# Gate and up of the 128-slot experts in blocks of 1024 columns over four PSUM banks

## The chip, the core and the metric

The kernel runs on one core of one Trainium2 chip, as one launch. The metric is the device time of that launch in microseconds (us), and each time named for a kernel is the median of several executions. The profiler took one more execution apart; its rows are used below. Engines are named as the profile names them: PE is TensorE, DVE is VectorE, ACT is ScalarE, POOL is GpSimd, and SP is SyncE, which here issues the weight transfers.

## What is computed

The reference is two stacks of transformer layers over 256 tokens of width 1024 in fp32. The change touches only the last feed-forward layer, a mixture of eight experts of which each token takes two:

```python
def swiglu_2(x, wg, wu, wd):
    return (jax.nn.silu(x @ wg) * (x @ wu)) @ wd

def moe_swiglu(x, router, wg, wu, wd):
    ...
    logits = (t @ router).astype(jnp.float32)
    top_v, top_i = lax.top_k(logits, TOP_K)
    ...
    for e in range(N_EXPERTS):
        y = y + gate[:, e:e + 1] * swiglu_2(t, wg[e], wu[e], wd[e]).astype(jnp.float32)
```

For each expert `wg` and `wu` are 1024 x 3584 and `wd` is 3584 x 1024, all fp32: 44.0 MB for an expert, 352 MB for the eight.

## The kernel before

**Jobs.** `moe` (line 2303) runs the eight experts one after the other in the order of `JOBS`: L, S, L, L, S, L, L, S. An L job has 128 slots for tokens (five experts), an S job 64 (three experts). The tokens of an expert are gathered by a selection matrix on PE, and its result is added back to the sum in the same way (`scatter`).

**An L job** (`job_l`, line 2371). Weights come in units of 128 x 1024 fp32, which is 512 KB. A unit lands in a raw buffer and is split by ACT (`hi`, rounded to fp32r) and DVE (`lo`, the rest). There are eight pairs of `hi` and `lo`. A product takes three fp32r matmuls of 512 columns: x hi by w hi, x hi by w lo, x lo by w hi. Gate and up are done by `stream_gu` (line 2257) in seven blocks j of 512 columns. A block takes two PSUM banks, one for gate and one for up, and 48 matmuls: eight k, three products, two weights. One unit holds 512 columns of two neighbouring k, so each of its rows of DRAM is 2 KB long. At a block's end ACT takes silu of the gate bank and DVE multiplies it by the up bank (`evac_gu`). A side task then transposes the result on PE in another bank and splits it. The down product is a `stream` of 28 units, 168 matmuls in two banks.

**An S job** uses the weights as they land, in fp32 matmuls on half of PE's columns (line 330). Its gate and up already come as units of 128 x 1024 of one k in three blocks, and as two-k units for the last 512 columns.

**Banks.** Of the eight PSUM banks four (`mq`) serve the main streams and four (`sm`) the side tasks: transposes, gathers, scatters. `lend(n)` (line 360) moves banks between the two.

**The order** of the instructions is fixed when the program is written out, by a planner in the kernel. It keeps a clock for PE, one for each other engine and one for the transfers, with a price for each operation; for the transfers it is 358e3 bytes a us (line 206). A matmul is written out when the planner thinks that its operands and its bank are ready (`pe` and `until`, line 263). Splits of units go into ACT's and DVE's queues up to 8 us (`AHEAD`) ahead of the planner's clock.

**Fillers.** Where the planner thinks that PE will stand idle for 1.2 us or more and a bank has been free for that long, `reach` (line 273) writes out matmuls of the identity, 128 x 128 in fp32, into a free bank: as many as cover the planned gap but for its last us. Nobody reads what they make. They are the matmuls of line 286:

```python
        while self.pe_end + 1.0 < self.clock:
            self.nc.tensor.matmul(ps[:, 0:128], self.c["ident"], self.c["ident"], start=True, stop=True)
            self.pe_end += 0.214
```

They are part of PE's queue, so PE runs them whether or not the gap is there on the chip.

Of the kernel before, what the change touches and what calls it, by code (L numbers as in the profile page):

```python
# [19 lines left out]
S, D, KD = 256, 1024, 8  # L20
# [95 lines left out]
class Net:  # L116
# [526 lines left out]
    def xf(self, t, k):  # L643
        self.wait(self.evs[t][k // 4])
        return self.xT[t][0][:, k], self.xT[t][1][:, k]
# [1367 lines left out]
    def plan_moe(self):  # L2013
        A = self.A

        g, u, d = (A[f"moe_w_{z}_2"][0].rearrange("e (c p) f -> p (e c) f", p=128) for z in ("gate", "up", "down"))
        self.m_val = {}

        def two(w, i, c, js):

            def get():
                b = self.expert(i)[0] if i is not None else None
                z = w[:, c:c + 2, js] if b is None else w[:, bass.ds(b + c, 2), js]
                return [z[:, 0, :], z[:, 1, :]], z
            return get

        def one(w, i, c, js, which):
            def get():
                b = self.expert(i)[which] if i is not None else None
                z = w[:, c:c + 1, js] if b is None else w[:, bass.ds(b + c, 1), js]  # L2030
                return [z[:, 0, :]], None
            return get

        for path, i in self.JOBS:
            plain = path == "S"
            for b in range(3 if plain else 0):
                for k in range(KD):
                    for w in (g, u):
                        self.unit(one(w, i, k, slice(b * 1024, b * 1024 + 1024), 0), plain=True)
            for j in range(6 if plain else 0, 7):  # L2040
                for k in range(0, KD, 2):
                    for w in (g, u):
                        self.unit(two(w, i, k, slice(j * 512, j * 512 + 512)), plain=plain)
            for k in range(28):
                self.unit(one(d, i, k, slice(0, 1024), 1), plain=plain)

# [199 lines left out]
    def stream(self, n, xf, evac):  # L2246
# [7 lines left out]
        evac(ps)  # L2254
        self.mq.put(2)

    def stream_gu(self, xf, evac):

        ps = self.new_mm()
        for k in range(KD):  # L2260
            if k % 2 == 0:
                ids = [self.take(), self.take()]
            xh, xl = xf(k)
            for a, (l, r) in enumerate(((xh, 0), (xh, 1), (xl, 0))):
                for z, i in enumerate(ids):
                    self.mm(ps[:, z * 512:z * 512 + 512], l, self.units[i][r][:, k % 2 * 512:k % 2 * 512 + 512],
                            k == 0 and a == 0, k == KD - 1 and a == 2)
            if k % 2:
                for i in ids:
                    self.done(i)  # L2270
            self.pump()
        evac(ps)
        self.mq.put(2)
# [29 lines left out]
    def moe(self, result, before):  # L2303
# [32 lines left out]
        def at_down(n, k):  # L2336

            if k == 12 and n < 7:
                path, i = self.JOBS[n + 1]
                self.spawn((self.gather if path == "L" else self.gather_s)(i, Gs[n + 1]))  # L2340
            if k == 10 and n == 7:
                wb.extend(before())
                self.wait(sev[6])
                self.grab(self.sm, 4)
                for t in range(2):
                    fin.append([self.new_sm() for _ in range(2)])
                    for h in range(2):
                        self.mm(fin[t][h], c["ident"], yacc[t][h], True, False)

        def scatter(n, lhs, yh, yl, back):  # L2350

            if n == 7:
                for t in range(2):
                    for h in range(2):
                        self.mm(fin[t][h], lhs(t, h), yh[h], False, False)
                        self.mm(fin[t][h], lhs(t, h), yl[h], False, True)
                self.fire(sev[n])
                return
            yield self.at(*yh, *yl)
            for t in range(2):  # L2360
                for h in range(2):
                    yield (self.sm, 1)
                    p2 = self.new_sm()
                    self.mm(p2, lhs(t, h), yh[h], True, False)
                    self.mm(p2, lhs(t, h), yl[h], False, True)
                    v.tensor_add(yacc[t][h], yacc[t][h], p2)
                    self.sm.put()
            self.blk.put(back)
            self.fire(sev[n])

        def job_l(n, G):
            hT, hev = [None] * 7, [Ev() for _ in range(7)]

            def xf(k):
                self.wait(G["ev"][k // 4])
                hi, lo = G["x"][k // 4]
                return hi[:, (k % 4) * 128:(k % 4) * 128 + 128], lo[:, (k % 4) * 128:(k % 4) * 128 + 128]

            def evac_gu(j):
                def go(ps):  # L2380
                    self.grab(self.blk, 2)
                    sg, h = self.new_blk(), self.new_blk()
                    nc.scalar.activation(sg, ps[:, 0:512], AF.Silu)
                    v.tensor_mul(h, ps[:, 512:1024], sg)
                    self.blk.put(1)

                    def tail():
                        yield self.at(h)
                        yield (self.blk, 2)
                        yield (self.sm, 1)  # L2390
                        hi, lo = self.new_blk(F32R), self.new_blk(F32R)
                        hv, lv = (z.rearrange("p (c t) -> p c t", c=4) for z in (hi, lo))
                        self.split_T(h, 4, hv, lv)
                        self.blk.put(1)
                        hT[j] = (hv, lv)
                        self.fire(hev[j])
                    self.spawn(tail())
                return go
            for j in range(7):
                self.stream_gu(xf, evac_gu(j))  # L2400
            self.blk.put(4)

            def hf(k):
                self.wait(hev[k // 4])
                at_down(n, k)
                hv, lv = hT[k // 4]
                if k % 4 == 3:
                    self.blk.put(2)
                return hv[:, k % 4], lv[:, k % 4]

            def evac_y(ps):
                self.wait(G["ev"][2])
                gs, sT = G["gs"], G["sT"]
                self.grab(self.blk, 4)
                yh = [self.new_blk(F32R) for _ in range(2)]
                yl = [self.new_blk(F32R) for _ in range(2)]
                for h in range(2):
                    sl = slice(h * 512, h * 512 + 512)
                    nc.scalar.activation(yh[h], ps[:, sl], AF.Copy, scale=gs)
                    v.scalar_tensor_tensor(yl[h], ps[:, sl], gs, yh[h].bitcast(F32), op0=OP.mult, op1=OP.subtract)  # L2420
                self.spawn(scatter(n, lambda t, h: sT[:, t * 128:t * 128 + 128], yh, yl, 5))
            self.stream(28, hf, evac_y)
# [320 lines left out]
```

## Time and profile before

| | us |
|---|---|
| median of 3 runs | 2643.92 |
| lowest and highest | 2642.69 and 2645.01 |
| the profiled execution | 2643.15 |
| its span, first to last instruction | 2641.4 |

The mean granted clock of PE in the profiled execution is 0.991 of full speed. The expert layer takes the last 950 us of the span: the first L job streams from 1693 to 1819 us, then S to 1914, two L to 2176, S to 2272, two L to 2534, and S to 2626. In the views, a window has for each engine the busy time and the count of records; an fp32 matmul leaves two records and an fp32r matmul one. A DMA share of 1 means that the 16 DMA engines were occupied all the time. The timeline gives start, length, engine, line, tiles and count of neighbouring equal instructions.

### The profile page before, as it was taken

What the parts mean: (1) busy time and instruction counts of PE and PEld (TensorE: products, weight loads), DVE (VectorE), ACT (ScalarE), POOL (GpSimd) and SP (SyncE); (2) the same over time, 40 slices, a digit from 0 to 9 for tenths busy, and PEclk for the clock granted to TensorE, in tenths of its full rate; (3) what the DMA queues carried; (4) which work ended last, traced back from release to release, by engine and by line L of the source; (5) the groups of instructions that cost most, each with busy time, mean ns of one, the idle gap of its engine ahead of it and who ended that gap; (6) DMA issues with size and microseconds to landing.
All of it is one profiled execution on the core that took longest, in us unless ns stands there. A gap on an engine that the chain in (4) does not pass through costs nothing.

```text
span 2641.4 us, 37877 instructions
## 1 busy us (share of the span) xinstructions
PE 2574.4 (97%) x12846; PEld 1989.5 (75%) x12846; DVE 1721.5 (65%) x2713; ACT 1291.1 (49%) x1827; POOL 130.2 (5%) x221
## 2 busy tenths in 40 slices
PE   8999989999999999999999999999999999999997
PEld 7887766788888888888878878886488884688853
DVE  6798866655655567556775578893098960698911
ACT  5644433454344455544544445582187750577710
POOL 1001124000000000000000010000000000000000
PEclk9999998999999999999999999999999999999999
DMA  6546868556356544464365553799999999999996
GB/s 220 158 154 214 256 219 281 175 168 228 118 180 203 156 135 153 159 200 144 104 207 172 194 158 117 239 388 363 355 386 393 380 336 403 389 391 343 368 351 271
DMA packets 309111, 649.10 MB, mean 246 GB/s; under 512 B 57194, under 2 KB 70856, under 8 KB 308912
## 3 DMA queue, kind: packets, MB, share of 16 engines
q1 hardware_dynamic: 295680, 608.23, 65.9%
q0 software_dynamic: 12560, 38.32, 4.5%
q8 instruction: 102, 1.67, 0.3%
q14 instruction: 97, 0.79, 0.1%
q10 hardware_dynamic: 672, 0.08, 0.0%
HBM read 635.03 MB, written 15.68 MB: 246 GB/s over the span
## 4 chain that ended last, share of the span: by engine, by line
PE 69%; DVE 6%; DMA 5%; issue 2%; ACT 2%; POOL 0%; SPq 0%; DVEq 0%; POOLq 0%; ACTq 0%
PE ps L338 57%; PE ps L330 7%; PE ps L343 4%; DVE blk L102 2%; PE ps L286 2%; DVE lo L102 2%; ACT hi L102 1%; DMA raw<-in_ffn_w_gate_up 1%; DVE x L102 1%; DMA lo<-in_moe_w_gate 1%; DMA blk<-s5E 1%; DMA hi<-in_moe_w_down 0%; DMA blk<-in_moe_w_gate 0%; DMA hi<-in_moe_w_gate 0%; ACT blk L102 0%
## 5 line engine op out<-in xcount | busy, mean ns | idle before, releaser
L338 PE MATMUL ps<-hi,blk 128*128 128x512 f32 x3024 | 842.7, 395 | 0.4 <-ACT blk L102 0.3
L102 DVE TENSOR_TENSOR lo<-raw,hi 128x1024 fp32r<-128x1024 f32 (+2 forms) x492 | 556.7, 1158 | 175.2 <-ACT hi L102 168.1
L338 PEld LDWEIGHTS ps<-hi,blk 128*128 128x128 f32 x3024 | 563.5, 188 | 129.0 <-issue 5.6
L102 ACT CAST hi<-raw 128x1024 fp32r<-128x1024 f32 (+2 forms) x492 | 479.3, 999 | 233.1 <-PE ps L338 201.6
L338 PE MATMUL ps<-lo,blk 128*128 128x512 f32 x1512 | 479.7, 395 | 0.0
L338 PE MATMUL ps<-lo,xh 128*128 128x512 f32 (+2 forms) x1296 | 417.9, 389 | 2.9 <-DVE lo L102 2.9
L338 PE MATMUL ps<-hi,xh 128*128 128x512 f32 (+2 forms) x1296 | 419.7, 390 | 1.0 <-ACT xh L102 0.9
L338 PE MATMUL ps<-hi,xl 128*128 128x512 f32 (+2 forms) x1296 | 418.2, 389 | 1.0 <-DVE xl L102 1.0
L102 DVE SCALAR_TENSOR_TENSOR lo<-raw,gam,hi 128x1024 fp32r<-128x1024 f32 (+3 forms) x272 | 303.0, 1135 | 79.4 <-ACT hi L102 68.5
L102 DVE TENSOR_TENSOR blk<-ps,blk 128x512 f32<-128x512 f32 (+4 forms) x220 | 139.9, 642 | 292.5 <-PE ps L330 152.1
L338 PEld LDWEIGHTS ps<-lo,blk 128*128 128x128 f32 x1512 | 282.6, 188 | 62.8 <-issue 1.4
L102 ACT ACTIVATE hi<-raw,gam 128x1024 fp32r<-128x1024 f32 (+3 forms) x272 | 275.9, 1032 | 90.0 <-PE ps L338 76.2
L338 PEld LDWEIGHTS ps<-hi,xl 128*128 128x128 f32 x1296 | 241.2, 189 | 48.8 <-DVE xl L102 2.0
L338 PEld LDWEIGHTS ps<-lo,xh 128*128 128x128 f32 x1296 | 239.2, 189 | 50.4 <-DVE lo L102 4.9
L338 PEld LDWEIGHTS ps<-hi,xh 128*128 128x128 f32 x1296 | 239.9, 189 | 48.6 <-issue 2.2
L343 PE MATMUL ps<-ident,blk 128*128 128x128 f32 (+3 forms) x957 | 152.8, 278 | 23.4 <-DVE blk L102 20.1
L343 PEld LDWEIGHTS ps<-ident,blk 128*128 128x128 f32 (+3 forms) x957 | 110.3, 137 | 84.1 <-DVE blk L102 44.7
L102 ACT CAST blk<-ps 128x512 fp32r<-128x512 f32 (+2 forms) x137 | 76.1, 556 | 168.3 <-PE ps L343 113.0
L338 PE MATMUL ps<-blk 128*128 128x64 f32 (+11 forms) x1104 | 143.1, 303 | 3.8 <-DVE blk L102 2.2
L102 ACT ACTIVATE blk<-ps 128x512 f32<-128x512 f32 (+1 forms) x75 | 41.7, 556 | 211.3 <-PE ps L330 144.7
L338 PEld LDWEIGHTS ps<-blk 128*128 128x128 f32 (+5 forms) x1104 | 117.8, 173 | 26.1 <-ACT blk L102 7.0
L102 DVE TENSOR_TENSOR lo<-old,hi 128x1024 fp32r<-128x1024 f32 x96 | 115.8, 1222 | 25.1 <-ACT hi L102 24.1
(273 smaller groups left out, 1977.1 us busy)
## 6 DMA issues: line engine op xcount, KB each, us to landing
raw<-in_ffn_w_gate_up SPq DMA_DIRECT2D x320, 256.0 KB, 4.3
raw<-in_ffn_w_down SPq DMA_DIRECT2D x110, 512.0 KB, 5.0
raw<-in_moe_w_down SPq DMA_DIRECT2D x105, 512.0 KB, 6.6
raw<-in_moe_w_gate SPq DMA_DIRECT2D x99, 512.0 KB, 7.1
raw<-in_moe_w_up SPq DMA_DIRECT2D x99, 512.0 KB, 7.3
blk<-in_moe_w_down SPq DMA_DIRECT2D x98, 256.0 KB, 6.0
old<-in_moe_w_gate SPq DMA_DIRECT2D x46, 512.0 KB, 9.3
blk<-in_moe_w_up SPq DMA_DIRECT2D x90, 256.0 KB, 6.8
```

The source lines that it names most:

```text
L102: return real(*a, **k)
L286: self.nc.tensor.matmul(ps[:, 0:128], self.c["ident"], self.c["ident"], start=True, stop=True)
L330: self.nc.tensor.matmul(out, lhsT, rhs, start=start, stop=stop)
L338: self.nc.tensor.matmul(out, lhsT, rhs, start=start, stop=stop)
L343: self.nc.tensor.transpose(out, in_, self.c["ident"][:p, :p])
```

## The change

An L job's gate and up are done in three blocks of 1024 columns and one of 512. `stream_gu2` holds four banks for a block, one gate and one up bank for each half of 512 columns. For each k it does the six matmuls of the first half, then the six of the second, on the same two units. At the last k the first half is evacuated right after its six matmuls, then the second half is done and evacuated. The next block's first half goes into two free banks, and its second half into the two banks that the old first half gave back. So that there are six banks for that, `lend(-2)` takes two of the side tasks' banks before the blocks, and `lend(2)` gives them back after. The units of these blocks hold 1024 columns of one k, with rows of 4 KB; units that land in pairs of half-width buffers are still moved as two transfers with rows of 2 KB. The last 512 columns stay with `stream_gu`. The number of units, matmuls, splits, evacuations and transfers stays the same, and so does the sequence of buffers that the units go to.

```diff
-            for b in range(3 if plain else 0):
+            for b in range(3):
                 for k in range(KD):
                     for w in (g, u):
-                        self.unit(one(w, i, k, slice(b * 1024, b * 1024 + 1024), 0), plain=True)
-            for j in range(6 if plain else 0, 7):
-                for k in range(0, KD, 2):
-                    for w in (g, u):
-                        self.unit(two(w, i, k, slice(j * 512, j * 512 + 512)), plain=plain)
+                        self.unit(one(w, i, k, slice(b * 1024, b * 1024 + 1024), 0), plain=plain)
+            for k in range(0, KD, 2):
+                for w in (g, u):
+                    self.unit(two(w, i, k, slice(3072, 3584)), plain=plain)
...
+    def stream_gu2(self, xf, evac):
+
+        ps = [self.new_mm(), self.new_mm()]
+        for k in range(KD):
+            ids = [self.take(), self.take()]
+            xh, xl = xf(k)
+            for h in range(2):
+                for a, (l, r) in enumerate(((xh, 0), (xh, 1), (xl, 0))):
+                    for z, i in enumerate(ids):
+                        self.mm(ps[h][:, z * 512:z * 512 + 512], l, self.units[i][r][:, h * 512:h * 512 + 512],
+                                k == 0 and a == 0, k == KD - 1 and a == 2)
+                if k == KD - 1:
+                    evac[h](ps[h])
+                    self.mq.put(2)
+                self.pump()
+            for i in ids:
+                self.done(i)
...
-            for j in range(7):
-                self.stream_gu(xf, evac_gu(j))
+            self.lend(-2)
+            for b in range(3):
+                self.stream_gu2(xf, [evac_gu(2 * b), evac_gu(2 * b + 1)])
+            self.stream_gu(xf, evac_gu(6))
+            self.lend(2)
```

In the rows that follow, `ps_` with a number is a PSUM bank in one use, `hi_` and `lo_` are the halves of a split unit, and `blk_` is a half-width tile.

PE in the first L job, before, where one block of 512 columns ends (banks 15395 and 15396) and the next begins (15496 and 15497):

```order
L338 MATMUL ps_15395<-hi_15375,blk_15214 128x512
L338 MATMUL ps_15396<-hi_15383,blk_15214 128x512
L338 MATMUL ps_15496<-hi_15409,blk_15200 128x512
L338 MATMUL ps_15497<-hi_15417,blk_15200 128x512
L338 MATMUL ps_15496<-lo_15410,blk_15200 128x512
L338 MATMUL ps_15497<-lo_15418,blk_15200 128x512
```

PE at the same point of the first L job, after, where block 0 (its second half in 15285 and 15286) ends and block 1 begins (first half 15487 and 15488, second half 15489 and 15490):

```order
L338 MATMUL ps_15286<-hi_15385,blk_15214 128x512
L338 MATMUL ps_15487<-hi_15405,blk_15200 128x512
L338 MATMUL ps_15488<-hi_15413,blk_15200 128x512
L338 MATMUL ps_15487<-lo_15406,blk_15200 128x512
L338 MATMUL ps_15488<-lo_15414,blk_15200 128x512
L338 MATMUL ps_15487<-hi_15405,blk_15201 128x512
L338 MATMUL ps_15488<-hi_15413,blk_15201 128x512
L286 MATMUL ps_15503<-ident_97 128x128 x26
L338 MATMUL ps_15489<-hi_15405,blk_15200 128x512
L343 MATMUL ps_15533<-ident_97,blk_15474 128x128 x4
L338 MATMUL ps_15490<-hi_15413,blk_15200 128x512
```

Between the six matmuls of the new first half and the first matmul of the second half, which needs a bank of the old block, 26 fillers now stand; before, no filler stood in this job.

PE in the third job (L), before, inside its first block:

```order
L338 MATMUL ps_17980<-lo_17911,blk_17725 128x512
L286 MATMUL ps_18009<-ident_97 128x128 x9
L338 MATMUL ps_17981<-lo_17947,blk_17725 128x512
L338 MATMUL ps_17980<-hi_17910,blk_17726 128x512
L338 MATMUL ps_17981<-hi_17946,blk_17726 128x512
```

PE in the third job, after, where its block 0 gives way to block 1:

```order
L338 MATMUL ps_18118<-hi_18028,blk_17760 128x512
L338 MATMUL ps_18119<-hi_18054,blk_17760 128x512
L286 MATMUL ps_18128<-ident_97 128x128 x11
L338 MATMUL ps_18120<-hi_18028,blk_17759 128x512
L343 MATMUL ps_18143<-ident_97,blk_18093 128x128 x4
L338 MATMUL ps_18121<-hi_18054,blk_17759 128x512
L343 MATMUL ps_18153<-ident_97,blk_18103 128x128 x4
L338 MATMUL ps_18120<-lo_18029,blk_17759 128x512
```

The nine fillers inside the block are gone, and eleven stand where the second half of block 1 needs a returned bank.

## Rows read from the trace of the kernel before

**Rows 1.** The page, busy time of PE over the whole span.

```profile
PE 2574.4 (97%) x12846; PEld 1989.5 (75%) x12846; DVE 1721.5 (65%) x2713; ACT 1291.1 (49%) x1827; POOL 130.2 (5%) x221
```

**Rows 2.** Windows by job: length; busy of PE, PEld, DVE, ACT, POOL; PEclk, DMA share, GB/s.

```profile
1693.00:1819.00 126.00, 125.33 (x582) 102.57 (x580) 104.67 (x147) 91.42 (x122) 0.00 (x0) 1.00 0.93 327
1819.00:1915.00 96.00, 91.16 (x470) 37.95 (x469) 10.86 (x17) 9.08 (x15) 0.00 (x0) 0.96 0.96 371
1915.00:2044.00 129.00, 129.00 (x606) 105.83 (x606) 116.30 (x132) 100.49 (x127) 0.00 (x0) 1.00 1.04 390
2044.00:2176.00 132.00, 132.00 (x640) 109.83 (x638) 105.29 (x124) 87.56 (x116) 0.00 (x0) 1.00 0.97 357
2273.00:2401.00 128.00, 128.00 (x599) 105.27 (x600) 111.81 (x127) 95.03 (x122) 0.00 (x0) 1.00 1.02 377
2401.00:2534.00 133.00, 133.00 (x644) 110.29 (x643) 106.32 (x125) 88.41 (x116) 0.00 (x0) 1.00 0.95 344
```

**Rows 3.** Waits of PE from 1693 to 2626 us: total, times, longest us.

```profile
PE ps L330 <- DMA raw<-in_moe_w_down: 4.8, 1, 4.8
PE ps L343 <- DVE blk L102: 1.8, 2, 0.9
PE ps L338 <- ACT blk L102: 0.7, 1, 0.7
```

**Rows 4.** Line 2502 (the branch in `overflow`): instructions of PE's sequencer, duration in ns.

```profile
L2502 PEldq COMPARE_BRANCH  x1: 6226/6226/6226, 1871.1 to 1871.1; - x1
```

**Rows 5.** Waits of SP, then of ACT, from 2273 to 2534 us (two L jobs).

```profile
SPq L102 <- DVE lo L102: 83.7, 107, 5.7
SPq L102 <- DMA raw<-in_moe_w_up: 11.7, 17, 0.8
...
ACT hi L102 <- PE ps L338: 42.3, 76, 2.5
```

**Rows 6.** Timeline of PE in the third job: start, length, engine, instruction, count.

```profile
1950.40 1.08 PE L338 MATMUL ps<-hi,blk 128*128 128x512 f32 x4
1951.32 0.63 PE L338 MATMUL ps<-lo,blk 128*128 128x512 f32 x2
1951.79 1.08 PE L338 MATMUL ps<-hi,blk 128*128 128x512 f32 x4
```

**Rows 7.** Windows, one of units with 4-KB rows, one of 2-KB rows.

```profile
1820.00:1840.00 20.00, 20.00 (x90) 7.30 (x88) 4.19 (x7) 1.33 (x3) 0.00 (x0) 1.00 1.03 409
1940.00:1960.00 20.00, 20.00 (x92) 16.33 (x91) 19.66 (x24) 16.01 (x22) 0.00 (x0) 1.00 1.05 386
```

**Rows 8.** Timeline of PE around the nine fillers of the third job.

```profile
1931.76 0.39 PE L338 MATMUL ps<-lo,blk 128*128 128x512 f32 x1
1931.99 2.17 PE L286 MATMUL ps<-ident 128*128 128x128 f32 x18
1933.92 0.47 PE L338 MATMUL ps<-lo,blk 128*128 128x512 f32 x1
1934.23 1.08 PE L338 MATMUL ps<-hi,blk 128*128 128x512 f32 x4
```

**Rows 9.** Windows of the fillers alone (line 286): length, busy of PE and PEld, PEclk, DMA.

```profile
1693.00:1819.00 126.00, 0.00 (x0) 0.00 (x0) 1.00 0.93 327
1915.00:2044.00 129.00, 3.60 (x28) 3.39 (x27) 1.00 1.04 390
```

**Rows 10.** Timeline of PE, ACT and DVE at a block's end in the seventh job.

```profile
2425.46 1.07 PE L338 MATMUL ps<-hi,blk 128*128 128x512 f32 x4
...
2426.84 1.04 ACT L102 CAST hi<-raw 128x1024 fp32r<-128x1024 f32 x1
2427.79 0.58 ACT L102 ACTIVATE blk<-ps 128x512 f32<-128x512 f32 x1
...
2428.12 1.22 DVE L102 TENSOR_TENSOR lo<-raw,hi 128x1024 fp32r<-128x1024 f32 x1
2429.25 0.68 DVE L102 TENSOR_TENSOR blk<-ps,blk 128x512 f32<-128x512 f32 x1
```

## The prediction

> **What bounds the kernel now.** Read first which engine is full. Over the span PE is 97% busy [rows 1], and in the windows of the L jobs it is 125.33 of 126 us, 129.00 of 129, 132.00 of 132, 128.00 of 128 and 133.00 of 133 [rows 2]. In the same windows the DMA share is 0.93 to 1.04, so transfers look just as full. A share cannot tell which of the two waits for the other; the waits can. From 1693 to 2626 us, all eight jobs, PE waited 7.3 us in three groups, and the one that is put down to a transfer, 4.8 us [rows 3], is at the place where PE's sequencer spent 6.2 us in the branch of the overflow code [rows 4]. So PE waits for no weights. The other side does wait: in the last two L jobs SP, which issues the transfers, waited 83.7 us for DVE to free a raw buffer, against 11.7 us in the largest group behind a transfer still under way, and ACT's splits waited 42.3 us for PE to free a `hi` buffer [rows 5]. The chain of cause runs from PE back to the transfers.
>
> Second, the pace. From 1950.40 to 1951.79 us PE starts six matmuls, 231.7 ns each [rows 6]. An L job has 504, so 116.8 us of its 126 to 133 us [rows 2] are these alone. The granted clock is 1.00 in all five L windows [rows 2], the level of 2.4 GHz. The L jobs are therefore as long as the list of what PE has been given to do. The S jobs are also run off in PE's written order, in which the change leaves every instruction as it was.
>
> **What the change removes.** Matmuls, splits, evacuations and transfers stay the same in number, so nothing goes there. Only the form of the transfers changes. With 4-KB rows 409 GB/s moved, with 2-KB rows 386 [rows 7]: a unit of 524,288 bytes takes 1.282 us instead of 1.358. In the first L job 34 of the 56 gate and up units get whole 4-KB rows, in the other four 36 each (the rest land in half-width buffers, or belong to the last 512 columns), 178 in all: 178 x 0.076 = 13.5 us of transfer time saved. I cost this at nothing, since SP then only waits longer for the same buffers [rows 5]. Just after an S job the lead of the weights is smallest, but PE waits for none there either [rows 3].
>
> The rows show 6% more bandwidth from rows of twice the length. The Trainium skill, "Perfetto Trace Analysis", section "DMA Optimizations", says that larger DMA sizes saturate HBM better and that going from 2 KB to 4 KB can improve throughput dramatically, as the primary step where a kernel is DMA-bound. The trace agrees on the direction (409 against 386 GB/s); by that rule this kernel would gain the 13.5 us, if transfers bound it. That is the first rival below.
>
> **What the change adds.** It adds fillers. Before, a block's two banks had a whole other block, 48 matmuls or 11.1 us, to be evacuated in. Now the second half of block 1 needs banks that the first half of block 0 gives back only 12 matmuls earlier. The planner thinks the banks come later than PE, and at each such place it writes fillers into PE's queue (the order rows under the change show two of them: 26 and 11).
>
> Counted in the programs, for the L jobs: the first had none and has 26 + 6. The first pair of L jobs had 9, 2, 3 and 24, and has 11, 6, 11, 6 and 24. The second pair had 9, 2 and 29, and has 12, 6, 16, 6 and 20. Two at the first pair's start stand in both. That is 32 + (58 - 38) + (60 - 40) = 72 more. The S jobs keep their 17, 42 and 29.
>
> What one costs is read where nine of them stand, 18 records [rows 8]. The matmul before them starts at 1931.76, so without fillers the third start from there would have been at 1931.76 + 2 x 0.23 = 1932.22; it is at 1934.23. Nine fillers cost 2.01 us, 0.223 us each. From their own start to the next matmul, 1931.99 to 1933.92, they took 0.214 each. From the busy time of all in the third job, 3.60 us for 28 records [rows 9], it is 0.257. I take 0.223, since it holds what happens to the next matmul's start: **72 x 0.223 = 16.1 us**, with 15.4 and 18.5 as ends. No cover hides them: PE is full on both sides, and the first L job with no filler at all loses nothing that they could fill [rows 9].
>
> **The wait itself.** Is the bank back when the fillers end? In the seventh job a block's last matmul starts at 2425.69 (the second of the four from 2425.46). ACT takes silu from 2427.79, after a split that ended only at 2427.88, and DVE ends its product at 2429.25 + 0.68 = 2429.93, after a split of 1.22 us [rows 10]. That is 4.24 us behind the last matmul's start. In the changed order, from the same point, the second half's six matmuls and the next block's first six begin 0.23 us later and take 12 x 0.2317 = 2.78 us, so fillers begin at 3.0 us. Six end at about 4.3 us, eleven at 5.5. So the bank is back at about the moment that six fillers end: 0 us of wait on top. If the evacuation stood one more split of 1.22 us back in DVE's queue, it would be back at 5.46 us: the five places with six fillers would wait some 1.2 us each, 6 us in all, and those with eleven or more would not wait. An evacuation that came at once would give nothing back, since the fillers are still run.
>
> The lent banks leave two for the side tasks. The scatter of the job before then needs its four banks in two turns. The program writes its later two parts 29 matmuls (6.7 us) or more further on, with no filler between, so I cost it at 0, within the 6 us above. Behind a PE that waits stands everything else of the job, since its queue is in order.
>
> **The sum.** Against the profiled execution: 2643.15 + 16.1 = 2659.2 us; its span would be 2641.4 + 16.1 = 2657.5. The median of the runs is 0.8 us above that execution, so I expect a median of 2660.0 us, 0.6% slower.
>
> **The rivals.**
>
> *Transfers bound the L jobs after all: faster.* For it: DMA share 1.04 and 1.02 in the two L jobs that follow an S job [rows 2]. Then the fillers would fall into waits for weights, and the 13.5 us would come off: 2643.9 - 13.5 = 2630.4. This decides from the point where a split waits for a landing and PE for the split. Against it: PE's list of waits has no such row in 933 us [rows 3], and PE's pace is even within a unit [rows 6]. The rule cited above is this rival's. Chance 0.05.
>
> *The fillers are swallowed: no change.* The 72 fillers would have to replace waits that PE has now. There are 7.3 us of those in all [rows 3], 4.8 of them in a branch in an S job that stays. If later jobs caught up through the weights' larger lead, the result would be within 5 us of 2643.9. PE's list has no slack that a lead could use. Chance 0.08. That the change doesn't do what it says is part of this one: 102 of the 280 units keep rows of 2 KB, which matters only if transfers bind.
>
> *Banks come late as well: slower still.* ACT and DVE are at 100.49 and 116.30 of 129 us in the third job [rows 2]; two evacuations in a row put 2 x 0.68 us of products on DVE at once. With one split more ahead of them at all ten places the waits come to 6 us, or with fillers at their dear end 18.5 + 6 = 24.5: 2666 to 2668. Chance 0.15.
>
> *The forecast:* 16 us of fillers and up to 3 us of waits, 2658 to 2663. Chance 0.72.
>
> **How the numbers follow.** The likeliest case gives 2660.0. From the two slower cases: their low end is 15.4 us of fillers, less the 4.8 us of rows 3 if a moved program should shorten that branch, 2643.9 + 10.6 = 2654.5; I go to 2652 for the spread between runs (2.3 us). Their high end is 2668, and 2670 with the same spread. The cases left out are the faster one and the one of no change, 0.13, and a small tail above. A measurement of this kernel can tell about 0.2%, 5.3 us, from no change. Faster by more than that: 0.05. Within it: 0.08. Slower: 0.15 + 0.72 = 0.87.
>
> **What the profile after would show.** Right: in the first L job's window line 286 has 64 records where it had none, about 7 us, and the window is as much longer. Each pair of L jobs is 261 + 4.5 us or so; the S jobs keep 96, 97 and 92 us. Six matmuls still take 1.39 us. GB/s rises while gate and up land, and SP waits longer for DVE. PE's waits in L jobs stay under 1 us each. Wrong: a wait of PE for ACT or DVE of over 1 us at each block's change (the third rival); L jobs no longer than now in spite of the 72 fillers (the second); a faster pace of the matmuls as the transfers get faster (the first). If the fillers ran faster than 0.2 us each, or S jobs got shorter, my sum would be wrong in its size.

## The result, and the profile after

| | before | after |
|---|---|---|
| median of six runs of each | 2644.03 us | 2661.2 us |
| lowest and highest | 2641.59 and 2645.01 | 2658.76 and 2665.22 |
| the profiled execution, its span | 2643.15, 2641.4 | 2658.76, 2657.0 |

The changed kernel is slower: the ratio after to before is 1.0067, with a 95% interval of [1.0056, 1.0078]. The forecast was 2660.0 us.

The medians lie 17.2 us apart, the spans of the two profiles 15.6. Part of such a difference is spread that the change doesn't make: in the fourteen profiles of this document the first L job begins anywhere from 1692.6 to 1700.1 us, though PE's instructions before it are the same, but for five fillers that experiments 6 and 7 leave out there. So differences of a few us are read below from the first L job's first matmul to the end of the span as well, called the expert layer's time: 948.0 us before, 964.4 after.

The first view to read is again the one of windows, now over the jobs as they lie in the changed kernel (columns as in [rows 2]: length; busy time of PE, PEld, DVE, ACT, POOL with counts; granted clock, DMA share, GB/s):

```profile
1693.00:1826.00 133.00, 132.32 (x642) 109.30 (x642) 104.99 (x147) 91.20 (x121) 0.00 (x0) 1.00 0.91 316
1826.00:1922.00 96.00, 91.25 (x469) 37.97 (x466) 13.32 (x19) 11.80 (x19) 0.00 (x0) 0.96 0.97 376
1922.00:2051.00 129.00, 129.00 (x614) 106.61 (x613) 114.22 (x130) 96.83 (x124) 0.00 (x0) 1.00 1.02 389
2051.00:2188.00 137.00, 137.00 (x674) 114.05 (x674) 107.09 (x125) 89.80 (x117) 0.00 (x0) 1.00 0.92 334
2284.00:2413.00 129.00, 129.00 (x613) 106.70 (x612) 112.06 (x127) 95.36 (x122) 0.00 (x0) 1.00 0.99 375
2413.00:2550.00 137.00, 137.00 (x673) 113.70 (x671) 107.22 (x125) 89.80 (x117) 0.00 (x0) 1.00 0.90 329
```

Where PE was full it is still full, at the same granted clock of 1.00; the windows are longer. Taken from first matmul to first matmul, so that no edge of a window blurs it:

| stretch | before | after | difference |
|---|---|---|---|
| first L job | 125.63 | 132.94 | +7.31 |
| S job behind it | 95.96 | 96.34 | +0.38 |
| first pair of L jobs | 261.33 | 265.88 | +4.55 |
| S | 96.57 | 96.58 | +0.01 |
| second pair of L jobs | 261.60 | 265.74 | +4.14 |
| last S, and the tail | 106.93 | 106.91 | -0.02 |

With a start that lies 0.77 us earlier these add up to +15.6 us, which is the whole of 2657.0 - 2641.4. Next, is it waiting or work? PE's waits from 1693 to 2645 us (total, times, longest), which answer [rows 3]:

```profile
PE ps L330 <- PEq L2522: 4.7, 1, 4.7
PE ps L343 <- DVE blk L102: 1.7, 2, 0.9
PE ps L338 <- ACT blk L102: 1.5, 2, 0.8
PE ps L338 <- DVE blk L102: 0.3, 1, 0.3
```

Waits come to 8.2 us now. Before, they came to 8.4 over the same stretch: the 7.3 us of [rows 3] end at 2626 us and miss 1.1 us in the tail. The largest is the branch in `overflow` again, this time put down to PE's sequencer and no longer to a transfer. By the timeline the others are at the gather in the first L job (0.68 us), in two S jobs and in the tail: not one is at a block's change. So the 15.6 us are work. The windows of line 286 alone (length, busy of PE and PEld, clock, DMA share, GB/s), to be held against [rows 9], show which:

```profile
1693.00:1826.00 133.00, 7.47 (x64) 7.46 (x64) 1.00 0.91 316
1922.00:2051.00 129.00, 4.86 (x40) 4.69 (x38) 1.00 1.02 389
```

The first L job has 64 records, 32 fillers, where it had none, and is 7.31 us longer. The matmuls that compute have kept their pace. PE's timeline in the third job (start, length, instruction, count):

```profile
1960.61 1.10 PE L338 MATMUL ps<-hi,blk 128*128 128x512 f32 x4
1961.54 0.63 PE L338 MATMUL ps<-lo,blk 128*128 128x512 f32 x2
1962.01 1.07 PE L338 MATMUL ps<-hi,blk 128*128 128x512 f32 x4
```

Six matmuls in 1.40 us, as in [rows 6]. And the transfers, faster by their longer rows, wait longer for the same buffers. SP's waits in the second pair of L jobs (2284 to 2550 us), which answer [rows 5]:

```profile
SPq L102 <- DVE lo L102: 110.0, 114, 9.5
SPq L102 <- DMA raw<-in_moe_w_up: 7.6, 11, 0.8
```

From 83.7 to 110.0 us, while the waits behind transfers under way got shorter. The stretch is also 5 us longer, so this pair of rows doesn't price the transfers by itself; experiment 1 does.

Last, what the fillers cover. This is PE, ACT and DVE where block 0 of the third job gives way to block 1 (brackets: idle before, and its releaser):

```profile
1944.70 1.09 PE L338 MATMUL ps<-hi,blk 128*128 128x512 f32 x4
...
1945.13 0.60 ACT L102 ACTIVATE blk<-ps 128x512 f32<-128x512 f32 x1 [0.33 <-PE ps L338]
...
1945.98 0.68 DVE L102 TENSOR_TENSOR blk<-ps,blk 128x512 f32<-128x512 f32 x1
1946.09 1.08 PE L338 MATMUL ps<-hi,blk 128*128 128x512 f32 x4
...
1946.52 0.60 ACT L102 ACTIVATE blk<-ps 128x512 f32<-128x512 f32 x1 [0.79 <-PE ps L338]
...
1947.15 0.69 DVE L102 TENSOR_TENSOR blk<-ps,blk 128x512 f32<-128x512 f32 x1 [0.49 <-ACT blk L102]
...
1947.48 0.63 PE L338 MATMUL ps<-hi,blk 128*128 128x512 f32 x2
...
1947.95 2.62 PE L286 MATMUL ps<-ident 128*128 128x128 f32 x22
...
1950.32 0.48 PE L338 MATMUL ps<-hi,blk 128*128 128x512 f32 x1
```

The first half's last matmul starts at 1944.93 (the second of the four from 1944.70). ACT, which stood idle for it, takes silu at 1945.13, and DVE's product is done at 1945.98 + 0.68 = 1946.66. The bank that the eleven fillers wait for is back 1.29 us before the first of them begins. The second half, whose last matmul starts at 1946.32, is evacuated by 1947.84, also before 1947.95. The fillers run from there, and the matmul that was ready all along starts at 1950.32. They cover nothing. At nine of the ten changes it is so: the first half's product is done 0.17 to 1.31 us before the first filler. Only at the very first, in the first L job, does it end 0.52 us after its 26 fillers have begun.

### The profile page after: what moved, and what is told of

Read it like the earlier page. It is cut to its first block, busy times and chain, and to the rows that moved or that the text cites. A ratio compares the mean times of both kernels' runs of the same rounds, so it can differ in the third digit from the quotient of the medians.

```text
span 2657.0 us, 38166 instructions
## 1 busy us (share of the span) xinstructions
PE 2589.3 (97%) x12990; PEld 2006.2 (76%) x12990; DVE 1724.8 (65%) x2713; ACT 1294.6 (49%) x1827; POOL 130.4 (5%) x221
## 5 line engine op out<-in xcount | busy, mean ns | idle before, releaser
L102 DVE TENSOR_TENSOR blk<-ps,blk 128x512 fp32r<-128x512 f32 (+4 forms) x220 | 138.4, 641 | 300.2 <-PE ps L330 152.1
L102 DVE TENSOR_TENSOR lo<-blk,hi 128x512 fp32r<-128x512 f32 x204 | 126.3, 684 | 1.9 <-ACT hi L102 1.6
```

Of the source, the lines that this page charges most:

```text
L102: return real(*a, **k)
```

## The experiments

All ratios are to the kernel before, run on the same chip beside the variant.

**1. Is the loss the transfers' form, or the order?** The changed order of work was given units with rows of 2 KB, and the order of before units with rows of 4 KB. PE's, ACT's and DVE's instructions stay in each case those of the kernel that was edited.

```diff
# a_2kb (changed kernel)
-   self.unit(one(w, i, k, slice(b * 1024, b * 1024 + 1024), 0), plain=plain)
+   self.unit(one(w, i, k, slice(b * 1024, b * 1024 + 1024), 0) if plain else
+             two(w, i, k // 2 * 2, slice((2 * b + k % 2) * 512, (2 * b + k % 2) * 512 + 512)), plain=plain)
# b_4kb (kernel before)
-   self.unit(two(w, i, k, slice(j * 512, j * 512 + 512)), plain=plain)
+   self.unit(two(w, i, k, slice(j * 512, j * 512 + 512)) if plain or j == 6 else
+             one(w, i, k + j % 2, slice(j // 2 * 1024, j // 2 * 1024 + 1024), 0), plain=plain)
```

> The changed kernel's order of instructions and its four banks, but each unit of the L jobs' blocks is read as two k of 512 columns, rows of 2 KB (other elements of the weights, the same bytes; so the L jobs compute something else). Theory: the transfers are hidden, 2661.2 us within 3. Rival (transfers bind): up to 13.5 us more, 2674.7 us.

> The kernel before in its order and with its two banks a block, but each unit of the L jobs' first six blocks is read as one k of 1024 columns, rows of 4 KB (other elements, the same bytes; so the L jobs compute something else). Theory: the transfers are hidden, 2644.0 us within 3, and SP waits longer for DVE to free buffers. Rival (transfers bind): 13.5 us less, 2630.5 us.

Measured: the changed order with 2-KB rows 2662.75 us, ratio 1.0065 [1.0051, 1.0079]; the old order with 4-KB rows 2644.96 us, 1.0002 [0.9993, 1.0011]. The form did change the bandwidth. One window of the third job in the first (2-KB rows) and in the second (4-KB rows):

```profile
1942.00:1962.00 20.00, 20.00 (x104) 16.77 (x103) 16.61 (x20) 14.14 (x20) 0.00 (x0) 1.00 1.05 387
```

```profile
1942.00:1962.00 20.00, 20.00 (x92) 16.29 (x92) 18.48 (x22) 15.84 (x22) 0.00 (x0) 1.00 1.03 402
```

387 GB/s against 402, PE at 20.00 of 20 us in both, and no time from it: the expert layer took 964.4 us with either length of row in the changed order, and 948.0 and 948.4 in the old one. With 4-KB rows in the old order SP waited 76.7 us for DVE from 1922 to 2171 us, against 60.7 before. Rows of 4 KB are worth nothing at this point, and the loss sits in the order alone. The Trainium skill, "Perfetto Trace Analysis", section "DMA Optimizations", puts going from 2 KB to 4 KB first where a kernel is DMA-bound. Here the bandwidth rose by 4%, and the time stayed, since the condition isn't met.

**2. Is it the fillers, and are the banks there without them?** In the changed kernel the fillers were left out where its blocks of 1024 run, 111 of them, and nothing else.

```diff
+            self.quiet = True
             for b in range(3):
                 self.stream_gu2(xf, [evac_gu(2 * b), evac_gu(2 * b + 1)])
+            self.quiet = False
...
-            self.nc.tensor.matmul(ps[:, 0:128], self.c["ident"], self.c["ident"], start=True, stop=True)
+            if not self.quiet:
+                self.nc.tensor.matmul(ps[:, 0:128], self.c["ident"], self.c["ident"], start=True, stop=True)
```

> The changed kernel with the fillers left out only where its blocks of 1024 columns run (111: the 106 at the ten block changes and five at a job's start); the 24 and 20 at the gathers of the S jobs stay. Theory as in the forecast (each filler at a block change costs 0.223 us and stands before a bank that is back already): 111 x 0.223 = 24.8 us less than 2661.2, so 2636.4 us, no wait of PE over 1 us at a block change, and the clock at 1.00 in the L jobs, since the half clock seen without any L fillers stood at the gathers alone. Rival (they stand in for a wait): PE waits of 1 us and more at the changes, up to 2661 us.

Measured: 2634.67 us, ratio 0.9961 [0.9948, 0.9975]. Against the changed kernel's 2661.2 that is 26.5 us. The expert layer's time fell from 964.4 to 939.5, by 24.8 us or 0.224 a filler, which is the theory's price. PE's waits from 1693 to 2620 us in it (line numbers lie 2 higher than in the changed kernel):

```profile
PE ps L332 <- PEq L2527: 4.7, 1, 4.7
PE ps L345 <- DVE blk L102: 1.9, 3, 0.9
PE ps L340 <- ACT blk L102: 1.5, 2, 0.8
```

Nearly the rows of the changed kernel: at all the blocks' changes together PE waits once, 0.19 us, at the first of them. The banks are back, and the fillers bought nothing there.

**3. What do the two lent banks do by themselves?** The kernel before, with only the lending around its seven blocks.

```diff
+            self.lend(-2)
             for j in range(7):
                 self.stream_gu(xf, evac_gu(j))
+            self.lend(2)
```

> The kernel before with its blocks of 512 columns in two banks, and only the two banks lent around gate and up of the L jobs. The planner then writes 17 fillers fewer in the two pairs of L jobs. Theory: 17 x 0.223 = 3.8 us less than 2644.7, so 2640.9 us, and lending itself is free. Rival (the side tasks suffer from two banks): 2645 us or more.

Measured: 2639.25 us, ratio 0.9978 [0.9969, 0.9987]. No loss of the side tasks with two banks shows. With more banks for the blocks the planner writes 17 fillers fewer, and 17 x 0.223 = 3.8 us lies within the interval (3.4 to 8.2 us). The expert layer got 5.4 us shorter, so some 1.6 us may have another cause, which no run here looks for.

**4. Are all fillers of the L jobs worthless?** All of them were left out of the L jobs, 155 in the changed kernel and 83 in the one before.

```diff
         for n, (path, _) in enumerate(self.JOBS):
+            self.quiet = path == "L"
             (job_l if path == "L" else job_s)(n, Gs[n])
```

> The changed kernel, with the fillers of the L jobs not written into PE's queue (155 of them, with the few at the jobs' edges); the planner still books their time, so all other instructions, banks and buffers stand as in the changed kernel. Theory (PE's list sets the L jobs, 0.223 us a filler, the banks are back in time): 155 x 0.223 = 34.6 us less than the changed kernel's 2661.2, so 2626.6 us, with no wait of PE for ACT or DVE of over 0.5 us where the blocks change. Rival (the fillers stand where PE would wait for the lent banks anyway): the time of the 106 fillers at the block changes comes back as waits of PE, so only the others save, some 49 x 0.223 = 10.9 us: 2650 us. Rival (transfers bind): above 2640 us, with waits for landings.

> The kernel before, with the fillers of the L jobs (83) not written into PE's queue. Theory: 83 x 0.223 = 18.5 us less than 2644.0, so 2625.5 us, and within 3 us of the changed kernel without its fillers: then blocks of 1024 columns, rows of 4 KB and lent banks are worth nothing by themselves and the whole loss of the change is fillers. Rival (transfers bind once PE is faster, the lead of the weights after an S job was 1.8 us at its smallest): slower than the changed kernel without fillers by up to 13.5 us, the transfer time that the 4-KB rows save.

Measured: 2633.34 us, 0.9959 [0.9945, 0.9973], for the changed kernel and 2636.76 us, 0.9961 [0.9947, 0.9974], for the one before. Both stayed behind the theory. The changed kernel gains 27.9 us, not 34.6, and only 1.3 us more than with 111 left out (2.9 in the expert layer). So the other 44, which stand in the down product where the tokens of the next S job are gathered, are worth most of their time. It is the first gather that needs them: from first matmul to first matmul the first pair of L jobs takes 257.62 us with its 24 and 257.51 without. The second pair takes 257.45 with its 20 and 253.92 without, where PE's wait at the gather is only 0.68 us. In the kernel before that second wait is 2.89 us and the pair takes 257.25, which is the 3.4 us between the two medians; the rival's transfers aren't needed to explain it. What the fillers did is seen where they are missing: PE's timeline in the kernel before without them, and two windows behind its wait.

```profile
2158.03 1.76 PE L340 MATMUL ps<-mopp,blk 128*128 128x1 f32 x8 [1.87 <-ACT blk L102]
2159.64 0.77 PE L340 MATMUL ps<-hi,blk 128*128 128x512 f32 x1
2160.22 1.05 PE L340 MATMUL ps<-lo,blk 128*128 128x512 f32 x2
2161.07 1.91 PE L340 MATMUL ps<-hi,blk 128*128 128x512 f32 x4
```

```profile
2160.00:2165.00 5.00, 5.00 (x13) 3.84 (x13) 2.35 (x3) 1.04 (x1) 0.00 (x0) 0.50 0.69 233
2165.00:2170.00 5.00, 5.00 (x23) 4.06 (x22) 0.15 (x1) 0.00 (x0) 0.00 (x0) 1.00 0.82 283
```

PE waits 1.87 us for ACT's cast, and behind that wait the granted clock falls to 0.50, the level of 1.2 GHz. Two matmuls then take 2161.07 - 2160.22 = 0.85 us, 425 ns each instead of 231.7. A window holds 13 records where the next, at 1.00, holds 23. The Trainium skill, "TensorE: Matmul & The Clock Gate", section "Wait — 56ns, not 53.3ns?", gives 426.7 ns for 512 columns at the low level, which agrees, and 215.7 ns at the high one, where this kernel takes 231.7.

**5. Without any filler in L and S jobs, do the 4-KB rows pay?** 243 fillers were left out of the changed kernel, 171 out of the one before.

```diff
         for n, (path, _) in enumerate(self.JOBS):
+            self.quiet = True
             (job_l if path == "L" else job_s)(n, Gs[n])
```

> The changed kernel with no fillers in the L and S jobs (243 left out). Theory: the 88 in the S jobs cost 0.223 us each as well, 19.6 us less than the 2633.3 us without the L jobs' fillers, so 2613.7 us, as long as weights keep up: the smallest lead at an L job's start, 5.2 us, falls by the 3.8 us of fillers of the first S job. Rival (S jobs without fillers wait for weights, and PE's clock falls in the waits): 2620 to 2640 us, with waits of PE for landings and a granted clock under 0.9 in the S jobs.

> The kernel before with no fillers in the L and S jobs (171 left out). Theory: 19.6 us less than its 2636.8 us without the L jobs' fillers, 2617 us, but its smallest lead was 2.3 us, less than the 3.8 us of fillers that go, so here rows of 2 KB begin to bind: 2 to 5 us slower than the changed kernel without fillers. Rival (transfers never bind): the same as the changed kernel without fillers within 3 us.

Measured: 2621.63 us, 0.9909 [0.9894, 0.9924], for the changed kernel and 2619.35 us, 0.9903 [0.9888, 0.9918], for the one before. The intervals lie on each other, so no gain from the 4-KB rows is seen. (In the two profiles the changed kernel's expert layer is 3.6 us the shorter, 920.6 against 924.2, but it began 6.4 us later, and in the pair of experiment 6 the two are 925.7 and 925.3.) Both theories missed, by 8 and 2 us. The changed kernel lies in its rival's range, but not by the rival's signs: the clock stayed at 0.96 or above in its S jobs, and PE's waits for landings came to 1.0 us, all in the last of them. In both new waits appeared. PE's waits in the kernel before so treated, from 1693 us on, and one place of PE's and DVE's timeline in the changed one:

```profile
PE ps L340 <- ACT blk L102: 6.2, 4, 2.9
PE ps L332 <- DMA raw<-in_moe_w_down: 4.8, 1, 4.8
PE ps L340 <- ACT hi L102: 4.6, 4, 2.1
```

```profile
2286.28 2.35 DVE L102 TENSOR_TENSOR lo<-old,hi 128x1024 fp32r<-128x1024 f32 x2
...
2286.41 0.85 PE L340 MATMUL ps<-hi,blk 128*128 128x512 f32 x3
...
2288.55 1.28 DVE L102 TENSOR_TENSOR blk<-ps,blk 128x512 f32<-128x512 f32 x2
...
2289.29 0.65 PE L345 MATMUL ps<-ident,blk 128*128 128x128 f32 x4 [2.02 <-DVE blk L102]
```

Of the 6.2 us 4.8 are the two gathers; the rest stood in the kernel before as well. The 4.6 us for ACT's `hi` are new: all four lie at the starts of the two L jobs behind an S job, where the split had only just been made. The last fence is the changed kernel's own weak point, at a block's change. DVE's products (2288.55) stand behind two splits of 2.35 us together, and PE waits 2.02 us for the first of them. That is the third rival's mechanism, with the difference that the instructions that wait are the transposes that read the product, which PE's queue has ahead of the matmul that needs the bank. It shows where the weights have next to no lead and splits are made at the last moment: by the landing records this job's second unit landed 0.5 us before the job's first matmul. Where blocks change it cost 0.83 us in the same run's third job and 0.67 in the changed kernel of experiment 6, and nowhere else more than 0.2.

**6. A dozen fillers at the gather.** No fillers in L and S jobs but at the gather, and each run of them cut at twelve.

```diff
-            self.nc.tensor.matmul(ps[:, 0:128], self.c["ident"], self.c["ident"], start=True, stop=True)
+            if not self.quiet and self.run < 12:
+                self.nc.tensor.matmul(ps[:, 0:128], self.c["ident"], self.c["ident"], start=True, stop=True)
+                self.run += 1
...
     def pe(self, out, ins, c):
+        self.run = 0
...
             for j in range(7):
                 self.stream_gu(xf, evac_gu(j))
+            self.quiet = False
...
+            self.quiet = True
             (job_l if path == "L" else job_s)(n, Gs[n])
```

> The kernel before, without fillers in the L and S jobs except at the two places in the L jobs' down product where the S job's tokens are gathered; there, and elsewhere, a run of fillers is cut to at most 12. Theory (the fillers at the gather stand for a wait of 1.8 us and then for matmuls at half clock, some 5.4 us a place; a dozen, 2.7 us, are enough to keep the clock): 2619.4 less 2 x 2.7, about 2614 us, and no half clock behind the gather. Rival (a dozen is too few: the wait stays, and the clock falls all the same): 2619 to 2622 us, with a granted clock of 0.5 to 0.7 behind the gather.

> The changed kernel, treated in the same way. Theory: where the fillers are gone, blocks of 1024 columns with 4-KB rows bring nothing, since the matmuls' own pace is the bound; in the changed kernel without any fillers the clock fell behind the gather in one of the two places only, so a dozen fillers there are worth less: 2619 to 2621 us, the same as or a little slower than the kernel before treated so. Rival (the 4-KB rows pay once nothing is spent on fillers): 2608 us or less, at least 5 us faster than the kernel before treated so.

Measured: 2620.91 us, 0.9911 [0.9895, 0.9928], for the kernel before and 2620.53 us, 0.9912 [0.9895, 0.9929], for the changed one. The theory's mechanism held, its sum didn't. In the kernel before so treated the wait at the gather is gone, but for 0.2 us at the second, and the clock behind it is 1.00; these are its windows behind the gather and at the starts of two L jobs, and its largest group of waits from 1905 to 2274 us:

```profile
2158.00:2163.00 5.00, 5.00 (x30) 4.29 (x29) 3.20 (x4) 1.63 (x2) 0.00 (x0) 1.00 0.75 221
```

```profile
1912.00:1922.00 10.00, 8.78 (x23) 6.30 (x24) 8.78 (x8) 8.30 (x11) 0.00 (x0) 0.66 1.03 379
2258.00:2268.00 10.00, 8.02 (x26) 5.95 (x27) 8.65 (x8) 8.18 (x9) 0.00 (x0) 0.83 1.05 386
```

```profile
PE ps L342 <- ACT hi L102: 5.6, 4, 2.5
```

The first pair of L jobs, first matmul to last, went from 259.95 (no filler) to 258.83 us, the second from 260.35 to 258.71. But the S job between them, up to the next L job's first matmul, went from 85.94 to 87.38 us, and the end from 84.28 to 86.05. What PE won there it lost in the S jobs and at the L jobs' starts. This is ACT and PE at the first of those starts:

```profile
1911.27 1.04 ACT L102 CAST hi<-old 128x1024 fp32r<-128x1024 f32 x1 [13.20 <-DMA old<-in_moe_w_gate]
```

```profile
1912.37 0.49 PE L342 MATMUL ps<-hi,blk 128*128 128x512 f32 x1 [2.54 <-ACT hi L102]
```

ACT has been idle for 13.20 us until the first unit lands, and PE waits for its split. At the second start ACT's wait is 13.74 us. The changed kernel came out where it was expected, but not for the expectation's reason, the matmuls' own pace: it too waits at both starts, 1.9 and 2.7 us.

**7. Are the weights now the bound?** Of the S jobs' down products 72 of 84 units were read by half, with everything else as in 6; the planner still books the whole transfer (`whole_bytes`), so the order of the instructions stays.

```diff
+                            cut = plain and self.down and pw == 1024
+                            self.whole_bytes = 524288 if cut else 0
+                            hi = 512 if cut else hi
                             nc.sync.dma_start(p[:, lo - po:hi - po], s[:, lo - o:hi - o])
...
-            self.mm_cols(ps[h * 64:h * 64 + 64, c:c + n], x, self.piece(i, o + h * n, o + h * n + n), start, stop)
+            z = 0 if self.same else o + h * n
+            self.mm_cols(ps[h * 64:h * 64 + 64, c:c + n], x, self.piece(i, z, z + n), start, stop)
```

> The kernel before with the gathers' dozen of fillers, and 72 of the 84 units of the S jobs' down products read by half only (512 of 1024 columns; both halves of the product use the same 512 columns, so the S jobs compute something else). PE's, ACT's and DVE's instructions are the same as without that; 18.9 MB of 352 are not moved. Theory (with so few fillers the S jobs run off the weights' lead, and the L job behind each waits for landings): the waits of 3.4 and 2.3 us at the two L jobs' starts and the half clock behind them go, and the S jobs get 1.8 to 3 us shorter: 2608 to 2613 us. Rival (the gain at the gather was lost in PE's own list): 2619 to 2622 us.

> The changed kernel treated in the same way. Theory: as the one before treated so, 2608 to 2613 us, since with its weights there in time PE's list is the same but for the place of its fillers. If 4-KB rows were worth something in the L jobs, the gap between this one and the changed kernel with whole transfers would be smaller than the same gap for the kernel before, by 3 us or more. Rival: 2619 to 2622 us.

Measured: 2604.83 us, 0.9855 [0.9838, 0.9871], and 2606.03 us, 0.9854 [0.9838, 0.9871]: 16.1 and 14.5 us less than with whole transfers, more than the 8 to 13 expected. In the kernel before the two pairs of L jobs got 4.2 and 3.4 us shorter, from first matmul to first matmul, and the S jobs and the tail 4.4, 2.3 and 2.5. PE's whole list of waits from 1905 to 2265 us in the kernel before so treated, and the two L starts' windows:

```profile
PE ps L348 <- DVE blk L102: 0.9, 1, 0.9
```

```profile
1908.00:1918.00 10.00, 10.00 (x44) 7.60 (x41) 8.30 (x12) 7.68 (x12) 0.00 (x0) 1.00 1.05 387
2248.00:2258.00 10.00, 10.00 (x46) 7.84 (x43) 8.41 (x11) 7.11 (x12) 0.00 (x0) 1.00 1.05 387
```

The waits at the starts are gone, PE is full and the clock is at its upper level, with the same PE instructions but for the columns that 72 of them read. So transfers do bind in experiment 6, at the way from an S job into the next L job: without fillers an S job takes PE some 85 us, and its 44.0 MB at 409 GB/s [rows 7] take 108. The rest has to come out of the lead that the L jobs have built up, and buffers limit that. Between whole and halved transfers lie 16.1 us for the kernel before and 14.5 for the changed one, too near to each other for the 4-KB rows to have been worth the 3 us of the expectation. A possible reason, not tested: 64 of the 84 units of an S job had 4-KB rows before.

## Why the prediction was right, step by step

**PE binds, not the transfers: right.** Both exchanges of the rows' length (experiment 1) moved bandwidth and not time. The 13.5 us of transfer time were rightly costed at nothing. The first rival is out for the kernel before. But the prediction didn't say how near it is: by the landing records the third job's first pairs of units, one of gate and one of up, were complete only 1.8 to 3.9 us ahead of their first matmul. With some 24 us taken off PE the rival holds (experiments 6 and 7), at 2619 to 2621 us.

**Seventy-two fillers at 0.223 us: right.** The sum said 16.1 us, the span shows 15.6, and the expert layer 16.4. By stretch it is 7.31 us for 32, 0.228 each; 4.55 for 20, 0.228; 4.14 for 20, 0.207. That the median, 2661.2, came within 1.2 us of the forecast is in part luck: the six runs of the changed kernel spread over 6.5 us.

**No wait beside them: right, by a wrong row.** The prediction took 4.24 us from a block's last matmul to its product's end [rows 10] and found the bank back as six fillers end. At the ten changes it was 1.7 us in the third and fourth jobs, 2.8 in the last pair, and 3.5 and 2.6 in the first job, so the bank was back before the first filler at nine of them. The row chosen was of a block with a split right ahead of each step of its evacuation. In the third and fourth jobs ACT was idle at the change, waiting for PE; in the other jobs silu did stand right behind a split, and in the last pair the margin was 0.17 us. The term was zero either way, as experiment 2 shows, but not by the prediction's sum. The third rival, 2666 to 2668 us at a chance of 0.15, rested on that row: no such wait came in the changed kernel, and waits of up to 2.02 us where the weights had lost their lead.

**"No cover hides them": right for the 72, wrong for fillers at the gathers.** The experiments that I built on the same price for every filler missed by 6.7 us (155 left out) and by 8 to 11 (83 left out: 18.5 expected, 8.0 by the medians and 10.3 by the ratio). The fillers at three of the four gathers (two in either kernel) stood for a wait of ACT's cast, and they kept the clock up; the changed kernel's second did without. A price per instruction holds where PE is full on both sides; it has to be looked at place by place.

**The lent banks at 0: right**, and by themselves a small gain (5.4 us of the expert layer), most of it fewer fillers.

**A faster version** than both is the kernel before without fillers in its L and S jobs, at 2619.35 us, 0.9903 [0.9888, 0.9918]. The two with a dozen fillers at the gather, and the changed kernel without any, can't be told from it.

## What to carry to other kernels

Where an order is written out ahead from a cost model, count what the model itself adds: a filler that is meant for a gap is executed whether or not the gap is there, and a change that only makes the model more cautious costs real time. Before paying for faster transfers see who waits in the rows of waits, not in the DMA share; a share of 1.05 stood beside a full PE and beside one that waited for weights. When the bound is loosened by 1%, look up the next one's distance first: here it was the lead of the weights after the S jobs, 2 us.

## What the runs showed of the hardware

A wait can cost more than itself. After PE's wait of 1.87 us at a gather the granted clock was 0.50 for the next window of 5 us, in which 13 records ran instead of 23. The length of the wait doesn't decide it alone. These are the windows around the wait of 2.02 us in experiment 5, at a block's change:

```profile
2287.00:2292.00 5.00, 2.98 (x18) 2.43 (x17) 5.00 (x6) 4.14 (x6) 0.00 (x0) 1.00 1.04 395
2292.00:2297.00 5.00, 5.00 (x24) 4.07 (x23) 5.00 (x8) 3.65 (x7) 0.00 (x0) 1.00 1.05 399
```

The clock stayed at 1.00, as it did behind a wait of 0.68 us at the changed kernel's second gather. What makes the difference was not tried. Twelve fillers, 2.84 us of PE's time, kept the clock at 1.00 behind the gather as well as the 24 that stood there before; other numbers were not tried.
